# First stage in one written order from the first band means, and a last MLP tile seeded in PSUM: a two-layer diffusion backbone on one core

## Chip, cores and metric

The kernel runs on one core of one Trainium2 chip. The metric is the device time of one execution in microseconds (us); lower is better. Data come in and go out in fp32; products of layers are computed from fp32 values split in a high and a low part of type fp32r (three products each: high by high, high by low, low by high).

## Reference

Two layers over 512 latent tokens (`x`) and 256 context tokens (`ctx`) of width 1024. Layer 0 mixes tokens by pooling, layer 1 by grouped-query attention; each is followed by a squared-ReLU MLP of inner width 4096. Every sub-layer has an RMS norm before and after it, and a shift, scale and gate that a linear map of the conditioning vector gives.

```python
def ada_mods(cond, w, b):
    m = (jax.nn.silu(cond) @ w + b)[..., None, :]
    return jnp.split(m, N_MOD, axis=-1)          # sh1, sc1, gt1, sh2, sc2, gt2

def pool_mixer(h, w_pool, pool_scale):           # windows 2, 4, 8, 16 for four groups of 256 columns
    ...
        mean = (jnp.take(csg, hi, axis=1) - jnp.take(csg, lo, axis=1)) / cnt
        diff = (mean - hf[..., sl]).astype(h.dtype)
        outs.append(diff @ w_pool[g])
    return jnp.concatenate(outs, axis=-1) * pool_scale

for i in range(2):
    h_lat = modulate(rms_norm(x, g_mix_pre[i]), sh1, sc1)          # the same for ctx
    y_lat = pool_mixer(...) if i == 0 else attention_mixer(...)
    x = x + gt1 * rms_norm(y_lat, g_mix_post[i])
    m_lat = sq_relu_mlp(modulate(rms_norm(x, g_mlp_pre[i]), sh2, sc2), w_mlp_in[i], w_mlp_out[i])
    x = x + gt2 * rms_norm(m_lat, g_mlp_post[i])                   # ctx likewise, in layer 0 only
return x
```

## The kernel before

Tokens lie in six tiles of 128 rows (`t` 0 to 3 latent, 4 and 5 context). TensorE (PE) multiplies, VectorE (DVE) and ScalarE (ACT) do the element work, GpSimd (POOL) takes powers for the norms, and SyncE (SP) issues all DMAs in one queue.

**First stage** (all lines of it are recorded as L87, the line of the helper that keeps program order). For each tile: load, `rows_a` (mean square on ACT, then `+ EPS` and the power -0.5 on POOL), `rows_b` (rows scaled, DVE), `band_mm` (products with banded matrices that give "window mean minus identity", PE, tiles `psm` of latent and `psc` of context columns), `band_ev` (out of PSUM, ACT or DVE). Column blocks are numbered `k` 0 to 7; `psm` and `psc` hold two of them. Beside this the conditioning runs: `ada_mm` multiplies a 1 MB load of `w_ada` with the conditioning vectors (tile `psada`), `ada_rows` transposes the result on DVE, `ada_sel` turns it into columns on PE, `ada_mods` adds the bias on DVE. Names such as `SC1_2` mean scale 1, columns from block 2 on; a load of width `w=4` covers four blocks and half of the inner dimension (`a` and `b` halves), one of width 2 covers two blocks and all of it. The products of the means with the pooling weights follow (`pool:t:g`, group `g` needs the blocks 2g and 2g+1, made by `hi:k` on ACT and `lo:k` on DVE), and the chain of each tile: mean square (`ms`), `rs`, copy out (`c`), gate (`b`), residual (`r`), mean square (`s`), `rs2`, scaling (`n`), transposes of tile pairs (`turn:t:q`), modulation (`h:t:q`), split in high and low part (`xhi`, `xlo`), and the first MLP products `in:t:q:f` (six matmuls of 256 columns each, `f` one of two PSUM tiles `psin`). The first unit of the MLP ends with `relu` of both `f`, and PE goes on with the next unit (L608).

Their order is a list by hand: `Steps` sorts the calls by a number `z`. Up to z = 24.5 the calls have their numbers in the code; from there the words of the string `FIRST` give them, one after the other. While `ordered` and `mixed` are on (z 0 to 100), PE, DVE and ACT carry out their instructions in exactly this program order; the SP queue takes its loads in this order as well. Four PSUM buffers `psB` (tag b) and two `psA` (tag a, two banks each) are shared; a tile waits until a buffer is free. Seven buffers take 1 MB loads.

**Middle.** MLP of layer 0, attention, MLP of layer 1 in a loop that is the same before and after; what is not pinned there is ordered by the compiler's own timing.

**Last MLP tile.** `finish` runs `out_mm` (products of the last two units, PE) and `out_ev` (L890: PSUM added to the accumulator `acc`, DVE) for each tile, then `norm_a` (L196: mean square of each column part, ACT; L207, L209, L211: sums and power, POOL), `norm_g` (L361: times gate, DVE) and `fin_b` (L364: residual, DVE; L1495: store). The last tile (`t` = 3) has three column parts, `THIRDS`: 512, 256 and 256 columns; PE does the parts one after the other.

Of the kernel before, what the change touches and what calls it, by code (L numbers as in the profile page):

```python
# [35 lines left out]
CONDITIONING = ((SC1, 0, 4), (SH1, 0, 4), (SC1, 2, 2), (SH1, 2, 2), (SC1, 3, 2), (SH1, 3, 2),  # L36
                (GT1, 0, 4), (GT1, 2, 4), (SC2, 0, 4), (SH2, 0, 4), (SC2, 2, 2), (SH2, 2, 2), (SC2, 3, 2), (SH2, 3, 2))
# [9 lines left out]
rows:GT1_2 ms:4:1 pool:0:2 gate:1:0 c:4:1 rs:4 sel:GT1_2 gate:0:0 pool:0:3 mods:GT1_2 gc:1:1 gc:0:1 whi:0 b:4:0  # L47
psg:1:1 pool:1:0 gate:1:1 wlo:0 psg:0:1 ms:0 b:5 pool:1:1 c:0* mm:SC2_0a rs:0 pool:1:2 r:5 ms:1:0 mm:SC2_0b
gate:0:1 b:4:1 pool:1:3 s:5 r:4 pool:3:0 pool:2:0 ms:1:1 rs2:5 b:0 mm:SH2_0a s:4 pool:3:1 rs:1 r:0 pool:2:1 n:5*
pool:2:2 rs2:4 b:1:0 mm:SH2_0b s:0 b:1:1 pool:3:2 r:1 pool:3:3 n:4* rs2:0 pool:2:3 rows:SC2_0 s:1 turn:4:0  # L50
rows:SH2_0 turn:4:1 sel:SC2_0 n:0* rs2:1 sel:SH2_0 mods:SC2_0 mods:SH2_0 mm:SC2_2 h:4:0 h:4:1* mm:SH2_2 n:1
xhi:4:1 rows:SC2_2 turn:0:0 xhi:4:0 xlo:4:1 turn:0:1 ms:3 xlo:4:0 sel:SC2_2 rows:SH2_2 h:0:0* mods:SC2_2 rs:3
# [38 lines left out]
def backbone(ctx: ExitStack, tc, x, ctx_in, w_ada, w_pool, pool_scale, w_qkv, g_q, g_k, w_o, w_mlp_in,  # L91
# [81 lines left out]
    HALVES, THIRDS = ((0, 512), (512, 512)), ((0, 512), (512, 256), (768, 256))  # L173

# [262 lines left out]
    for v, c in ((0, HALO), (1, P)):  # L437
        ve.tensor_copy(bands[:, v], bands[:, 2])
        ve.tensor_copy(bands[:, v, :, c:c + HALO], edges[:, v])

    means, lat, con = {}, {}, {}

    def band_open(k):
        lat[k] = psA.tile([P, 2, 512], F32, tag="a", name="psm")
        con[k] = psB.tile([P, 2, 256], F32, tag="b", name="psc")
        for u in range(2):
            means[k + u] = lat[k][:, u, :], con[k][:, u, :]
# [18 lines left out]
    def rows_a(t):  # L466
        rs[t] = row_rstd(xr[:, t, :])
# [21 lines left out]
    def pool_weights():  # L489
        for h in range(2):  # L490
            ps = psB.tile([P, 512], F32, tag="b", name="psg")
            te.matmul(ps, one[0:1, 0:1].broadcast_to([1, P]), scale_row[:, 512 * h:512 * h + 512], start=True, stop=True)
            pw.append(ps)
# [308 lines left out]
    def both(ks):  # L802
        for t in range(NL, NT):
            band_mm(t, ks)
# [782 lines left out]
```

## Time and profile before

| what | value |
|---|---|
| median of 3 runs (lowest to highest) | 1163.33 us (1163.19 to 1163.43) |
| time of the profiled execution | 1161.48 us |
| its span (first to last instruction) | 1159.7 us |
| instructions | 15945 |
| busy: PE / DVE / ACT / POOL | 1140.7 / 932.7 / 628.8 / 69.2 us |
| first product of the second MLP unit (L608, end of the first stage on PE) | 96.88 us |
| last residual begins (L364) | 1155.34 us |

A row of the timeline has: start in us, duration in us, engine, line, operation, output<-input, shape, xcount, and in brackets the idle time of the engine before it with what ended it. Rows on one line merge neighbouring instructions of one form. A row of groups has busy time in us and mean ns of one, then idle time before. `PEld` is the weight load of PE, which runs beside its matmuls. Durations of matmuls overlap, since they are pipelined: from start to start is what one costs.

### The profile page before, as it was taken

What the parts mean: (1) busy time and instruction counts of PE and PEld (TensorE: products, weight loads), DVE (VectorE), ACT (ScalarE), POOL (GpSimd) and SP (SyncE); (2) the same over time, 40 slices, a digit from 0 to 9 for tenths busy, and PEclk for the clock granted to TensorE, in tenths of its full rate; (3) what the DMA queues carried; (4) which work ended last, traced back from release to release, by engine and by line L of the source; (5) the groups of instructions that cost most, each with busy time, mean ns of one, the idle gap of its engine ahead of it and who ended that gap; (6) DMA issues with size and microseconds to landing.
All of it is one profiled execution on the core that took longest, in us unless ns stands there. A gap on an engine that the chain in (4) does not pass through costs nothing.

```text
span 1159.7 us, 15945 instructions
## 1 busy us (share of the span) xinstructions
PE 1140.7 (98%) x6172; PEld 990.7 (85%) x6172; DVE 932.7 (80%) x1515; ACT 628.8 (54%) x1068; POOL 69.2 (6%) x120
## 2 busy tenths in 40 slices
PE   7999999999999999999999999999999999999997
PEld 5679889998898988998888889998988888888886
DVE  4688588998988997996777699867687679778876
ACT  5676555554354534555675367753676436534522
POOL 2130000000000000000242200001100000000001
PEclk9999999999999999999999999999999999999999
DMA  9964222443334444343422102125334214313212
GB/s 374 418 270 151 73 99 87 146 145 131 123 145 146 146 146 145 109 146 109 182 73 73 37 1 74 37 74 168 122 146 146 81 64 146 109 44 138 109 41 104
DMA packets 25516, 147.32 MB, mean 127 GB/s; under 512 B 2785, under 2 KB 5217, under 8 KB 9698
## 3 DMA queue, kind: packets, MB, share of 16 engines
q1 hardware_dynamic: 25442, 146.32, 34.4%
q8 instruction: 48, 0.79, 0.3%
q14 instruction: 26, 0.21, 0.1%
HBM read 138.96 MB, written 7.34 MB: 126 GB/s over the span
## 4 chain that ended last, share of the span: by engine, by line
PE 62%; issue 30%; DVE 2%; POOL 2%; ACT 2%; DMA 1%; POOLq 0%; SPq 0%; DVEq 0%; ACTq 0%
PE pso L878 22%; PE psin L732 18%; PE psy L1403 3%; PE po L1378 3%; PE pss L1337 3%; PE psq L1133 2%; PE pspt L1359 2%; PE pspool L87 2%; PE psin L87 1%; PE psin L608 1%; PE psada L87 1%; DMA raw<-in_w_ada 1%; PE psm L87 1%; POOL rs L211 1%; PE psg L87 1%
## 5 line engine op out<-in xcount | busy, mean ns | idle before, releaser
L878 PE MATMUL pso<-units,rb 128*128 128x512 f32 x1152 | 278.8, 392 | 0.0
L878 PEld LDWEIGHTS pso<-units,rb 128*128 128x128 f32 x1152 | 214.7, 188 | 41.1
L301 DVE SCALAR_TENSOR_TENSOR rows<-raw,cond,rows 128x256 f32<-128x256 f32 x280 | 127.2, 478 | 2.0
L890 DVE TENSOR_TENSOR acc<-acc,pso 128x512 f32<-128x512 f32 x129 | 85.4, 676 | 40.5 <-PE pso L878 40.3
L608 PE MATMUL psin<-ra,rb 128*128 128x512 f32 (+1 forms) x310 | 87.8, 360 | 0.0
L987 PE MATMUL pso<-units,pairs 128*128 128x512 f32 x336 | 82.6, 389 | 0.0
L608 PE MATMUL psin<-ra 128*128 128x512 f32 (+1 forms) x256 | 76.5, 376 | 0.0
L987 PEld LDWEIGHTS pso<-units,pairs 128*128 128x128 f32 x336 | 63.1, 188 | 13.1
L991 DVE TENSOR_TENSOR acc<-acc,pso 128x512 f32<-128x512 f32 x72 | 48.7, 682 | 26.2 <-PE pso L987 26.2
L732 PE MATMUL psin<-ra,units 128*128 128x384 f32 x336 | 65.6, 337 | 0.4 <-ACT psin L744 0.4
L209 POOL TENSOR_SCALAR ms<-ss 128x1 f32<-128x1 f32 x16 | 8.7, 541 | 936.6 <-ACT junk L196 922.9
L732 PE MATMUL psin<-sums,units 128*128 128x384 f32 x336 | 64.0, 336 | 0.0
L732 PEld LDWEIGHTS psin<-ra,units 128*128 128x128 f32 x336 | 59.9, 188 | 3.9 <-ACT psin L744 0.5
L608 PEld LDWEIGHTS psin<-ra,rb 128*128 128x128 f32 x310 | 55.6, 189 | 8.7
L169 DVE TENSOR_TENSOR units<-raw,units 128x1024 fp32r<-128x1024 f32 (+2 forms) x49 | 55.1, 1152 | 8.6 <-ACT units L166 8.4
L732 PEld LDWEIGHTS psin<-sums,units 128*128 128x128 f32 x336 | 58.9, 188 | 1.6
L608 PE MATMUL psin<-rb 128*128 128x512 f32 (+1 forms) x155 | 55.8, 361 | 0.6 <-DVE rb L1472 0.6
L166 ACT CAST units<-raw 128x1024 fp32r<-128x1024 f32 (+2 forms) x49 | 46.9, 996 | 17.0 <-PE pso L878 12.9
L608 PEld LDWEIGHTS psin<-ra 128*128 128x128 f32 x256 | 47.1, 188 | 8.8
L888 ACT COPY acc<-pso 128x512 f32<-128x512 f32 x48 | 27.1, 586 | 46.9 <-PE pso L878 46.4
L1133 PE MATMUL psq<-units,ra 128*128 128x512 f32 x216 | 52.2, 393 | 0.0
L608 PE MATMUL psin<-rb,ra 128*128 128x512 f32 (+1 forms) x128 | 48.1, 376 | 0.0
(284 smaller groups left out, 2385.5 us busy)
## 6 DMA issues: line engine op xcount, KB each, us to landing
raw<-in_w_ada SPq DMA_DIRECT2D x48, 1024.0 KB, 5.2
raw<-in_w_mlp_in SPq DMA_DIRECT2D x32, 1024.0 KB, 4.9
raw<-in_w_mlp_out SPq DMA_DIRECT2D x32, 1024.0 KB, 5.8
raw<-in_w_qkv SPq DMA_DIRECT2D x6, 1024.0 KB, 4.9
spill<-xr SPq DMA_DIRECT2D x10, 512.0 KB, 4.3
xr<-spill SPq DMA_DIRECT2D x10, 512.0 KB, 6.7
raw<-in_w_o SPq DMA_DIRECT2D x4, 1024.0 KB, 4.8
xr<-in_x SPq DMA_DIRECT2D x4, 512.0 KB, 5.3
```

Source lines behind the costliest of these rows:

```text
L87: return lambda *args, **kw: self.tc.keep_in_program_order(f(*args, **kw))
L166: a = sc.copy(hi, raw)
L169: b = ve.tensor_tensor(out=lo, in0=raw, in1=hi, op=ALU.subtract)
L301: ve.scalar_tensor_tensor(out=r, in0=raw[:, k, :], scalar=cond[:, k, c:c + 1], in1=r, op0=ALU.mult, op1=ALU.add)
L608: te.matmul(ps[:, bank, o:o + ln], w[:, k, fs], rhs, start=start, stop=(k == KT - 1 and n == 2), skip_group_check=len(ks) < KT or self.paired)
L732: te.matmul(bank, w[k], a[k], start=start and k == 0 and m == 0, stop=stop and k == 3 and m == 2, skip_group_check=True)
L878: te.matmul(pss[h][:, 0:cols[h][1]], a[:, f, ts_], w[:, f, cols[h][0]:sum(cols[h])], start=(n == 0 and not seeded[t]), stop=(n == len(seq) ...
L890: ve.tensor_tensor(out=d, in0=d, in1=ps[:, 0:w], op=ALU.add)
L987: te.matmul(ps, a, w, start=(m == 0), stop=(m == len(seq) - 1))
L991: ve.tensor_tensor(out=M[n][:, t], in0=M[n][:, t], in1=ps, op=ALU.add)
L1133: te.matmul(ps, a[:, k, sl], w[:, k % 4, :], start=(k == 0 and n == 0), stop=(k == KT - 1 and n == 2))
L1337: te.matmul(ps[:, c2, 0:384], a[:, sl], b[:, kv, 384 * c2:384 * c2 + 384], start=(n == 0), stop=(n == 2))
```

## The change

1. *First stage.* `FIRST` now begins at z = 14.5, with the first evacuation of band means (`ev:0`), and has another order. New words: `rb`, `psc0`, `psm`, `psc`, `ev`, `evc` (rows, band products and their evacuations) and `wsc`, `wph`, `wpl` (pool weights scaled and split).
2. `SC1` and `SH1` are loaded for two blocks at a time throughout (`SC1_0`, `SC1_1` in place of `SC1_0` with halves a and b). Bytes and number of loads are the same, the pool weights are now loaded ahead of them.
3. `rows_a` adds `EPS` on DVE in place of POOL, within DVE's program order. Matrices for the last context tile (`band_edge(1)`) are made after two tiles in place of at once; the product that spreads the pool scale (`pool_weights`) is split, half 0 at the start, half 1 between the band products of tiles 1 and 2. `psm` and `psc` are opened apart.
4. *Last tile.* `seeded` is true for it: ACT copies its three parts of `acc` into PSUM ahead of the products, which accumulate on them. `out_ev` does nothing for it. Mean squares and gate products read PSUM; the sum of the three mean squares is one POOL instruction for the first two and one ACT instruction (Identity with a bias) for the third, then the power on POOL.
5. Its residual and store are in parts of 640 and 384 columns (512 and 512 before).

Columns 512, 256 and 256 are the parts that the tile had before as well (`LAST` has the value of `THIRDS`). The diff, with the old list cut:

```diff
-CONDITIONING = ((SC1, 0, 4), (SH1, 0, 4), (SC1, 2, 2), (SH1, 2, 2), (SC1, 3, 2), (SH1, 3, 2),
-                (GT1, 0, 4), (GT1, 2, 4), (SC2, 0, 4), (SH2, 0, 4), (SC2, 2, 2), (SH2, 2, 2), (SC2, 3, 2), (SH2, 3, 2))
+CONDITIONING = ((GT1, 0, 4), (GT1, 2, 4), (SC2, 0, 4), (SH2, 0, 4),
+                (SC2, 2, 2), (SH2, 2, 2), (SC2, 3, 2), (SH2, 3, 2))
 FIRST = """
-psc45 ev6 mm:SH1_0a ev4c psc67 mm:SH1_0b ev6c rows:SH1_0 mm:SC1_2 sel:SH1_0 rows:SC1_2 mods:SH1_0 sel:SC1_2 hi:0
-mods:SC1_2 mm:SH1_2 hi:1 lo:0 hi:2 rows:SH1_2 lo:1 mm:SC1_3 hi:3 sel:SH1_2 lo:2 pool:5:0 pool:4:0 rows:SC1_3
-mods:SH1_2 sel:SC1_3 lo:3 hi:5 mm:SH1_3 mods:SC1_3 hi:4 pool:5:1 rows:SH1_3 lo:5 sel:SH1_3 mm:GT1_0a pool:4:1
-mods:SH1_3 lo:4 hi:6 pool:0:0 pool:0:1 hi:7 lo:6 mm:GT1_0b pool:5:2 ms:4:0 lo:7 pool:4:2 c:4:0* rows:GT1_0
-mm:GT1_2a pool:5:3 sel:GT1_0 ms:5 pool:4:3 mods:GT1_0 gc:1:0 gc:0:0 psg:1:0 c:5* rs:5 mm:GT1_2b w_in psg:0:0
...
-rs2:2 sel:SH2_3 mods:SC2_3 in:0:2:0 mods:SH2_3 h:4:3 in:0:2:1 n:2* h:0:3 in:4:2:1 xhi:4:3 turn:2:0 turn:2:1
-xhi:0:3 xlo:4:3 turn:2:2 h:2:1* h:2:0 turn:2:3 in:4:3:0 xhi:2:1 xlo:0:3 in:4:3:1 xhi:2:0 xlo:2:1 in:0:3:0 h:2:2*
-xlo:2:0 in:2:1:0 h:2:3 xhi:2:2 in:2:0:0 in:2:0:1 xlo:2:2 xhi:2:3 in:2:1:1 xlo:2:3 in:2:2:1 in:0:3:1 in:2:2:0
-in:2:3:0 in:2:3:1
+ev:0* ev:2 psc0:4 psm:4 rb:5 wsc:0 psm:6 wsc:1 ev:4* wph:0 mm:SC1_0 wph:1 wpl:0 mm:SH1_0 ev:6* rows:SC1_0 wpl:1
+psc0:5 sel:SC1_0 rows:SH1_0 evc:2* mods:SC1_0 evc:0* sel:SH1_0 mm:SC1_1 mods:SH1_0 hi:0 psc:4 rows:SC1_1 hi:1
+psc:6 lo:0 mm:SH1_1 evc:4* lo:1 evc:6* sel:SC1_1 rows:SH1_1 pool:4:0 mods:SC1_1 sel:SH1_1 mm:SC1_2 mods:SH1_1
+hi:2 pool:0:0 rows:SC1_2 pool:5:0 hi:3 lo:2 mm:SH1_2 lo:3 sel:SC1_2 rows:SH1_2 pool:4:1 mods:SC1_2 sel:SH1_2
+ms:4:0 mm:SC1_3 mods:SH1_2 hi:4 c:4:0 pool:5:1 rows:SC1_3 mm:SH1_3 hi:5 lo:4 sel:SC1_3 pool:0:1 rows:SH1_3
+mods:SC1_3 sel:SH1_3 lo:5 pool:1:0 pool:1:1 mods:SH1_3 pool:5:2 hi:6 mm:GT1_0a ms:1:0 lo:6 pool:4:2 hi:7
+mm:GT1_0b c:1:0 lo:7 pool:0:2 mm:GT1_2a rows:GT1_0 pool:4:3 sel:GT1_0 ms:4:1 mm:GT1_2b w_in mods:GT1_0 gc:0:0
+gc:1:0 c:4:1* rs:4 pool:0:3 rows:GT1_2 psg:0:0 ms:0 sel:GT1_2 psg:1:0 c:0* mods:GT1_2 rs:0 gc:0:1 gc:1:1 psg:1:1
+gate:1:0 gate:0:0 pool:5:3 b:4:0 gate:1:1 b:1:0 mm:SC2_0a ms:5 b:4:1 psg:0:1 r:4 c:5* rs:5 pool:1:2 gate:0:1 b:5
+mm:SC2_0b s:4 pool:1:3 r:5 whi:0 rs2:4 pool:3:0 ms:1:1 rows:SC2_0 pool:3:1 c:1:1* b:0 mm:SH2_0a rs:1 n:4*
+sel:SC2_0 b:1:1 mm:SH2_0b s:5 r:0 pool:2:0 whi:1 rs2:5 pool:2:1 rows:SH2_0 pool:2:2 s:0 mods:SC2_0 r:1 sel:SH2_0
+mm:SC2_2 n:5* rs2:0 mods:SH2_0 wlo:0 pool:2:3 s:1 turn:4:0 n:0 turn:4:1 ms:2 rs2:1 mm:SH2_2 h:4:1 h:4:0* rs:2
+pool:3:2 n:1 xhi:4:0 mm:SC2_3 rows:SH2_2 xhi:4:1 rows:SC2_2 xlo:4:0 sel:SH2_2 turn:0:1 xlo:4:1 sel:SC2_2 h:0:1*
+pool:3:3 mods:SH2_2 mods:SC2_2 turn:0:0 b:2 xhi:0:1 mm:SH2_3 ms:3 xlo:0:1 in:4:0:1 h:0:0* rows:SH2_3 rs:3
+in:4:1:1 b:3 xhi:0:0 in:0:1:1 r:3 turn:0:2 in:4:0:0 h:0:2* xlo:0:0 in:4:1:0 s:3 r:2 in:0:1:0 in:0:0:1 xhi:0:2
+rs2:3 wlo:1 s:2 in:0:0:0 turn:0:3 xlo:0:2 n:3* sel:SH2_3 rs2:2 turn:4:2 rows:SC2_3 in:0:2:0 mods:SH2_3 h:4:2*
+n:2 sel:SC2_3 in:0:2:1 xhi:4:2 mods:SC2_3 turn:2:2 h:0:3 turn:4:3 h:2:2* turn:2:3 xlo:4:2 turn:2:1 xhi:2:2 h:4:3
+in:4:2:1 h:2:1* in:4:2:0 xlo:2:2 xhi:4:3 h:2:3 turn:2:0 in:2:2:1 xhi:2:1 xlo:4:3 xhi:0:3 in:2:2:0 xlo:2:1 h:2:0*
+in:4:3:1 xlo:0:3 in:2:1:0 xhi:2:0 xhi:2:3 in:0:3:1 xlo:2:0 xlo:2:3 in:0:3:0 in:4:3:0 in:2:0:0 in:2:3:0 in:2:0:1
+in:2:3:1 in:2:1:1
 """
+    LAST = ((0, 512), (512, 256), (768, 256))
 ...
     def rows_a(t):
-        rs[t] = row_rstd(xr[:, t, :])
+        ss, ms, rs[t] = sm_tile("ss"), sm_tile("ms"), sm_tile("rs")
+        mean_square(xr[:, t, :], ss[:, 0:1])
+        ve.tensor_scalar(out=ms[:, 0:1], in0=ss[:, 0:1], scalar1=EPS, scalar2=None, op0=ALU.add)
+        gp.tensor_tensor(out=rs[t][:, 0:1], in0=ms[:, 0:1], in1=nhalf[:, 0:1], op=ALU.pow)
 ...
+    st.at(0.1, pool_weights, 0)
+    for k in (0, 2):
+        st.at(1, band_open, k)
+        st.at(1, band_open_c, k)
     for t in range(NT):
         st.at(4.6 + 1.3 * t, rows_a, t)
-    for t, z in enumerate((7.8, 9.7, 11.2, 12.7, 14.2, 16)):
-        st.at(z, rows_b, t)
 ...
+    for t in range(NL + 1):
+        st.at(5.5 + 1.3 * t, rows_b, t)
     for t in range(NL):
+        st.at(5.6 + 1.3 * t, band_mm, t, range(4))
+    st.at(7.9, pool_weights, 1)
+    st.at(6.85, band_edge, 1)
+    st.at(14, pool_load)
 ...
-        st.at(24.5 + n / 1000, step, what)
+        st.at(14.5 + n / 1000, step, what)
 ...
-        seeded[t] = i == 0 and parts[0][0] > 0 and len(parts) == 1 and t in (1, 4) and stale[0] <= 0
+        seeded[t] = cols == LAST or i == 0 and parts[0][0] > 0 and len(parts) == 1 and t in (1, 4) and stale[0] <= 0
 ...
-                sc.copy(ps, accv[:, t, c0:c0 + w])
+                sc.copy(ps[:, 0:w], accv[:, t, c0:c0 + w])
 ...
     def out_ev(i, parts, t, cols=HALVES):
+        if cols == LAST:
+            return
 ...
+    def last_rstd(t, ss):
+        ms, rs[t] = sm_tile("ms"), sm_tile("rs")
+        for n, (c0, w) in enumerate(LAST):
+            mean_square(pso[t][n][:, 0:w], ss[:, n:n + 1])
+        gp.tensor_scalar(out=ms[:, 0:1], in0=ss[:, 0:1], scalar1=ss[:, 1:2], scalar2=EPS, op0=ALU.add, op1=ALU.add)
+        sc.activation(ms[:, 1:2], ss[:, 2:3], AF.Identity, scale=1.0, bias=ms[:, 0:1])
+        gp.tensor_tensor(out=rs[t][:, 0:1], in0=ms[:, 1:2], in1=nhalf[:, 0:1], op=ALU.pow)
 ...
     def norm_g(t, pool=False, cols=HALVES):
         yg[t] = work_tile()
-        for c0, w in cols:
-            z = gated(t, yg[t], accv[:, t, c0:c0 + w], c0, c0 + w, pool)
-            if cols == THIRDS:
+        for n, (c0, w) in enumerate(cols):
+            z = gated(t, yg[t], pso[t][n][:, 0:w] if cols == LAST else accv[:, t, c0:c0 + w], c0, c0 + w, pool)
+            if cols == LAST:
                 tc.keep_in_program_order(z)
 ...
-        for n0, n1 in ((0, 512), (512, D)):
+        c = 640 if t == NL - 1 else 512
+        for n0, n1 in ((0, c), (c, D)):
```

More of the change, by code (lines that the diff above doesn't have):

```diff
@@ L48 @@
[L48 to L52, printed above, removed]
@@ L436, in backbone, with band_edge @@
     edges = gflat[:, 12 * BW:12 * BW + 64].rearrange("p (v g n) -> p v g n", v=2, g=4)
-    for v, c in ((0, HALO), (1, P)):
+    def band_edge(v):
+        c = (HALO, P)[v]
         ve.tensor_copy(bands[:, v], bands[:, 2])
         ve.tensor_copy(bands[:, v, :, c:c + HALO], edges[:, v])
+    band_edge(0)
     means, lat, con = {}, {}, {}
@@ L444, in band_open, with band_open_c @@
         lat[k] = psA.tile([P, 2, 512], F32, tag="a", name="psm")
+        for u in range(2):
+            means[k + u] = lat[k][:, u, :], None
+    def band_open_c(k):
         con[k] = psB.tile([P, 2, 256], F32, tag="b", name="psc")
         for u in range(2):
-            means[k + u] = lat[k][:, u, :], con[k][:, u, :]
+            means[k + u] = means[k + u][0], con[k][:, u, :]
     def band_mm(t, ks):
@@ L487, in backbone, with pool_weights @@
     pw = []
[L489 to L493, printed above, removed]
+    def pool_weights(h):
+        ps = psB.tile([P, 512], F32, tag="b", name="psg")
+        te.matmul(ps, one[0:1, 0:1].broadcast_to([1, P]), scale_row[:, 512 * h:512 * h + 512], start=True, stop=True)
+        pw.append(ps)
     def pool_load():
@@ L797, in conditioning, with band_rows, band_context @@
         m, j = dict(SH1=SH1, SC1=SC1, GT1=GT1, SH2=SH2, SC2=SC2)[m], int(j[0])
-        w = 4 if j == 0 or m == GT1 else 2
+        w = 4 if m == GT1 or j == 0 and m in (SC2, SH2) else 2
         zs = (("ab".index(what[-1]),),) if w == 4 and fn == ada_mm else ()
         fn(0, m, j, *((w, *zs) if fn == ada_mm else ()))
-    def both(ks):
+    def band_rows(k):
+        band_open(k)
+        for t in range(NL):
+            band_mm(t, (k, k + 1))
+    def band_context(k):
+        band_open_c(k)
         for t in range(NL, NT):
-            band_mm(t, ks)
+            band_mm(t, (k, k + 1))
     def split_w(h, part):
@@ L823, in backbone @@
     kinds = dict(
-        psc45=lambda: both((4, 5)), psc67=lambda: both((6, 7)), ev6=lambda: band_ev(6, 0, True),
-        ev4c=lambda: band_ev(4, 1, True), ev6c=lambda: band_ev(6, 1, True),
+        rb=rows_b, psc0=lambda t: band_mm(t, range(4)), psm=band_rows, psc=band_context,
+        ev=lambda k, act: band_ev(k, 0, act), evc=lambda k, act: band_ev(k, 1, act),
+        wsc=pool_scaled, wph=lambda h: pool_split(h, True), wpl=lambda h: pool_split(h, False),
         mm=lambda x: conditioning(ada_mm, x), rows=lambda x: conditioning(ada_rows, x),
@@ L1174, in norm_a @@
         ss = sm_tile("ss")
+        if cols == LAST:
+            return last_rstd(t, ss)
         for n, (c0, w) in enumerate(cols):
@@ L1497, in last1 @@
     def last1(st, n, t):
-        cols = THIRDS if t == NL - 1 else HALVES
+        cols = LAST if t == NL - 1 else HALVES
         st.at(5.2 * n + 5.3, norm_a, t, cols)
```

25 lines of the change are left out of this document (3 added, 22 removed).

## Prediction

> **What bounds the kernel now.** I read the page first, then PE's waits, then the windows of ten us, then the rows at both ends of the run.
>
> ```profile
> span 1159.7 us, 15945 instructions
> ...
> PE 1140.7 (98%) x6172; PEld 990.7 (85%) x6172; DVE 932.7 (80%) x1515; ACT 628.8 (54%) x1068; POOL 69.2 (6%) x120
> ```
>
> PE is busy all but 19 us. In the profiled execution (1161.48 us, 1.8 beyond its span; the median of the runs is 1.85 above it) only two places can give time back without taking work from PE: the first stage and the tail. PE's waits from 8.6 to 97 us (total, times, longest):
>
> ```profile
> PE psada L87 <- DMA raw<-in_w_ada: 2.5, 3, 1.4
> PE psada L87 <- DVE mods L87: 1.5, 3, 0.7
> PE psada L87 <- ACT acc L87: 0.7, 1, 0.7
> PE psin L608 <- ACT work L615: 0.2, 1, 0.2
> ```
>
> That is 4.9 us, the ceiling for a mere change of order. The same view from 97 to 1150 us has five rows that sum to 2.2 us, the first and last of them:
>
> ```profile
> PE pss L1337 <- ACT gate L1342: 0.6, 2, 0.4
> ...
> PE psin L608 <- ACT work L615: 0.2, 1, 0.2
> ```
>
> So PE goes on without a break once the stage is over, and what it gains at the start should arrive at the end. The stage's other limit is DMA (columns: PE, PEld, DVE, ACT, POOL busy, clock, DMA share, GB/s):
>
> ```profile
> 60.00:70.00 10.00, 9.78 (x107) 7.14 (x109) 6.11 (x11) 7.36 (x13) 3.91 (x9) 1.00 1.01 417
> 70.00:80.00 10.00, 9.27 (x120) 6.98 (x113) 9.96 (x19) 9.45 (x18) 2.28 (x4) 1.00 0.21 83
> ```
>
> Loads run at full rate until about 70 us: 1.05 MB each, so 2.5 us apart at 417 GB/s. Neither their number nor the rate changes, so their landing times are given.
>
> **First stage: the waits taken out.** PE's rows in order of time:
>
> ```profile
> 31.07 1.07 PE L87 MATMUL psada<-raw,cond 128*32 128x256 f32 x16 [0.62 <-DMA raw<-in_w_ada]
> 33.55 1.07 PE L87 MATMUL psada<-raw,cond 128*32 128x256 f32 x16 [1.41 <-DMA raw<-in_w_ada]
> 34.41 0.25 PE L87 MATMUL psada<-rows,sel 128*32 128x4 f32 x8
> ```
>
> ```profile
> 42.86 1.69 PE L87 MATMUL pspool<-rb,ra 128*128 128x256 f32 x12
> 44.49 1.06 PE L87 MATMUL psada<-raw,cond 128*32 128x512 f32 x8
> ```
>
> A load's product costs 1.0 us, a pooling group (6 of the 12 matmuls that fill 42.86 to 44.49) 0.8, a turn into columns (`sel`) 0.25. PE waits for loads here because it has nothing else to do: the old `SC1_0` and `SH1_0` need two loads each before any block has its scale and shift. In the new list blocks 0 and 1 have both after the second conditioning load, so pooling groups stand between the later loads.
>
> A load that PE waited for landed when its row starts: `SH1_2` at 31.07, `SC1_3` at 33.55, and 2.5 later, at 36.05, `SH1_3`. That holds in the new order too, as the same nine loads (pool weights and eight of `SC1` and `SH1`) come first in both. After `SH1_3` the new list has its product 1.0, two turns 0.5, groups 0:1, 1:0, 1:1 and 5:2 3.2 (at 40.75), then `GT1_0a`, 4:2, `GT1_0b`, 0:2, `GT1_2a`, 4.6 more: done at 45.35, with eleven groups behind it. Before, `GT1_2a` is done at 45.5 (44.49 and 1.0) with eight. The lead is three groups and 0.15 us, 2.5 us, provided PE is ready for `SH1_3` when it lands. Two turns more than before (`SC1_1`, `SH1_1`, 0.5 us) are in this.
>
> **First stage: what is added at its start.** PE's rows:
>
> ```profile
> 4.98 3.75 PE L87 MATMUL psg<-work,sm 1*128 1x512 f32 x4 [4.98 <-DMA work<-in_pool_scale]
> 8.66 6.60 PE L87 MATMUL psm<-gate,acc 128*128 128x136 f32 x32
> 15.10 1.09 PE L87 MATMUL psc<-gate,acc 128*128 128x136 f32 x8
> ```
>
> The weight loads of one tile's eight band products, from the row of PEld:
>
> ```profile
> 10.19 1.99 PEld L87 LDWEIGHTS psm<-gate,acc 128*128 128x128 f32 x8
> ```
>
> And the rows of x on DVE, the power on POOL, the first copy of means on ACT, and, for want of a one-column add on DVE, its nearest row, the reciprocal of one column:
>
> ```profile
> 12.52 0.75 DVE L87 TENSOR_SCALAR acc<-xr,rs 128x1024 f32<-128x1024 f32 x1 [0.76 <-POOL rs L211]
> 14.04 0.75 DVE L87 TENSOR_SCALAR acc<-xr,rs 128x1024 f32<-128x1024 f32 x1 [0.77 <-POOL rs L211]
> ```
>
> ```profile
> 13.44 0.57 POOL L211 TENSOR_TENSOR rs<-ms,nhalf 128x1 f32<-128x1 f32 x1
> ```
>
> ```profile
> 14.83 1.01 ACT L87 COPY acc<-psm 128x1024 f32<-128x1024 f32 x1 [1.11 <-PE psm L87]
> ```
>
> ```profile
> L1348 DVE RECIPROCAL sm<-sm 128x1 f32<-128x1 f32 x32 | 5.1, 158 | 1.3 <-ACT gate L1342 0.3 <-ACT acc L1342 0.3 <-ACT p L1342 0.3
> ```
>
> Rows of x come 1.52 us apart now. With the add of `EPS` on DVE in program order, tile t+1's add stands behind tile t's scaling and ahead of its own: a chain of add 0.16, power 0.57, scaling 0.75 and hand-overs, 1.55 to 1.65 us a tile. What waits behind the add on DVE is the scaling, and for that PE waits. Tile 3 comes 0.1 to 0.4 us later by this, and by up to 0.75 (bounded by a scaling) for `band_edge(1)`, which now lies between tiles 1 and 2; in return tile 0 no longer has it ahead.
>
> PE is slower yet. Eight weight loads took 1.99 us at 10.19, while the eight `psc` products of 15.10 have full pace, 0.12 each (1.09 with the last one's run-out): PE is at half pace until about 13 us, though the clock column of the windows shows 1.00 from the start. The spreading product costs 0.94 a matmul cold (3.75 for four). New order: tile 0 from 8.4, tile 1 until 12.4 cold, `pool_weights(1)` until 13.4 if warm or 14.3 if cold, tiles 2 and 3 about 1.0 each until 15.3 to 16.2, against the copy's start at 14.83. I take 1.0 us late, from the middle of the two. About half of it comes through, since the landings at 31 to 36 us stay: the lead is 2.0 us. Bounds: 0.2 lost, or a PE that stays cold through tile 3, which is the first rival.
>
> [...]
>
> **First stage: its end.** From 45 us on both lists hold the same products, and PE is full but for 1.2 us (two of the waits for `mods`, 1.0, and L615's 0.2).
>
> ```profile
> 86.10 1.91 PE L87 MATMUL psx<-ident,acc 128*128 128x128 f32 x16
> 87.76 8.87 PE L87 MATMUL psin<-ra,rb 128*128 128x256 f32 x72
> 96.88 16.91 PE L608 MATMUL psin<-ra,units 128*128 128x384 f32 x96 [0.25 <-ACT work L615]
> ```
>
> Twelve `in` products take 8.7 us, 0.72 each; a transpose pair of `turn` 0.42 (1.66 for four). The wait ahead of L608 goes: `f` 0 now ends with three products of `f` 1 behind it, 2.2 us in which ACT can empty it, where one product, 0.72, left 0.25 open. The waits for `mods` may go or come back elsewhere; I count nothing. Stage: 2.0 and 0.25, say 2.3 us, L608 at 94.6. Bounds: 0 and 4.4 (every wait less the two turns).
>
> **The tail.** What stands around the last tile on DVE and ACT, then its own chain:
>
> ```profile
> 1146.62 1.37 DVE L890 TENSOR_TENSOR acc<-acc,pso 128x512 f32<-128x512 f32 x2 [0.76 <-PE pso L878]
> ```
>
> ```profile
> 1147.40 0.63 ACT L196 ACTIVATE junk<-acc 128x512 bf16<-128x512 f32 x1 [4.04 <-DVE acc L890]
> ```
>
> ```profile
> 1152.88 0.42 DVE L890 TENSOR_TENSOR acc<-acc,pso 128x256 f32<-128x256 f32 x1 [0.51 <-PE pso L878]
> ```
>
> ```profile
> 1153.44 0.42 ACT L196 ACTIVATE junk<-acc 128x256 bf16<-128x256 f32 x1
> ```
>
> ```profile
> 1154.11 0.55 POOL L209 TENSOR_SCALAR ms<-ss 128x1 f32<-128x1 f32 x1 [0.15 <-POOL ss L207]
> 1154.75 0.56 POOL L211 TENSOR_TENSOR rs<-ms,nhalf 128x1 f32<-128x1 f32 x1
> 1155.34 1.42 DVE L364 SCALAR_TENSOR_TENSOR xr<-work,rs,xr 128x512 f32<-128x512 f32 x2 [0.76 <-POOL rs L211]
> ```
>
> From PE's last product (1152.88) to the residual (1155.34) lie 2.46 us: add, square, sum, power. New: the square reads PSUM at once, from 1152.93; its sum is there 0.62 later (0.67 from 1153.44 to POOL's start, less a hand-over). Then the one-column Identity on ACT in place of POOL's 0.55: no row shows it just so; it lies between the reciprocal's 0.16 and the square's 0.42, and I take 0.2, near the former for its one column. 1152.93 + 0.62 + 0.2, a hand-over of 0.05, power 0.56 and 0.03 put the residual at 1154.4: 0.9 us gained. Residual and store are as long in sum; the last store is a quarter smaller, counted at nothing. Bounds 0.3 to 1.2.
>
> The seeds are three ACT copies, 0.63, 0.42 and 0.42 by ACT's rows of these widths. ACT's idle 4.04 us before 1147.40 covers the first two; the third needs a buffer that DVE frees from 1146.62 on, and has two parts' products ahead of it. Without that cover, the first seed queued behind tile 2's square, PE would stand still for 1.8 us at about 1147.
>
> Square and gate product of a part now read one PSUM tile. In the view of the tile `psy`, whose parts are read by both as well, ACT's squares waited for DVE's gate products (us, times):
>
> ```profile
>   ACT junk L196: 11.7, 6
> ```
>
> [...] Here the square is written first, and the gate product has until 1154.4: I count none of it.
>
> Sum: 2.3 + 0.9 = 3.2 us. The profiled 1161.48 becomes 1158.3, the median 1163.33 becomes 1160.1. A measurement of this kernel can tell about 0.2% (2.3 us) from no change, so faster is below 1161.0.
>
> **Rivals.**
>
> *Cold clock* (0.17). PE stands idle for 1.5 us after the first spreading product, the second one (one row of PE wide) falls into the middle, and PE isn't released before tile 3 is done. Tiles 2 and 3 cost 2.0 each: first means at 18.3, 2.1 us later than I take, of which 1.6 comes through. Stage 0.7, with the tail 1.6: 1161.7. For it: the spreading products ahead of 8.66 didn't warm PE. Against it: dense work from 8.4 to 12.4.
>
> *Only the tail gains* (0.12). PE comes to each load late and the lead is lost: 1162.4; the seeds' stall would do as much in another place. Against it: the eleven groups' operands need no load after `SH1_3`.
>
> *Slower* (0.13), by the row chain of tile 3, whose last pooling group now stands behind `SC2_3`.
>
> ```profile
> 65.03 2.42 PE L87 MATMUL pspool<-rb,ra 128*128 128x256 f32 x18
> ```
>
> ```profile
> 47.39 1.05 PE L87 MATMUL psg<-ident,gc 128*128 128x128 f32 x8
> ```
>
> Before, this group ends at 67.4 and the pair's transposes begin at 86.10, 18.7 us later. New: from 45.35 and 0.5 for the start, thirteen groups, eight loads, six turns, four gate spreads (1.0 each) and four transposes put it at 71.5. Fourteen `in` products and five transposes, 12.2 us, stand from `turn:2:2` on, so that decides from 84.7. With the old 18.7 us it begins at 90.2, L608 at 102.4: 5.5 later, less the tail's 0.9: 1167.9. For it: DVE and ACT are 99% and 94% busy from 70 to 80. Against it: much of the 18.7 was queueing behind other tiles, and `ms:3`, `b:3` and `r:3` now follow the product closely; I expect 81 to 82.
>
> That the change of order does nothing is no rival: the order is binding on PE, DVE and ACT.
>
> **Numbers.** Forecast 0.58, cold clock 0.17, tail alone 0.12, slower 0.13. Some nine in ten of the forecast's cases (stage 1.5 to 4) and a few of the cold ones lie below 1161.0: faster 0.57, same 0.30, slower 0.13. The range leaves out the slower rival and the last of the ceiling: 1158.0 to 1163.4.
>
> **What would show it.** Right: the first copy of `psm` near 16 us; no wait of PE for `in_w_ada` above 0.5 us; L608 near 94.6; the residual 1.5 us behind PE's last product; no L890 in tile 3. Wrong: weight loads at half pace beyond 14.5 us; PE waiting for `acc` ahead of tile 2's transposes; L878 waiting for ACT in the last tile; new waits of PE between 97 and 1150 us.

## The result and the profile after

The changed kernel takes 1159.99 us in the median of 12 runs (1157.69 to 1161.33), the kernel before 1163.01 us beside it (12 runs, 1161.78 to 1164.28). The ratio is 0.9971, 95% interval 0.9963 to 0.998: 3.0 us less. The profiled execution of the changed kernel took 1160.61 us, with a span of 1158.8. From the page:

```profile
span 1158.8 us, 16048 instructions
...
PE 1142.9 (99%) x6220; PEld 992.7 (86%) x6220; DVE 932.9 (81%) x1522; ACT 632.8 (55%) x1076; POOL 69.7 (6%) x113
```

PE has 2.2 us more busy time than before and the span is 0.9 us shorter. PE's waits from 4 to 97 us show what has gone:

```profile
PE psg L89 <- DMA work<-in_pool_scale: 5.1, 1, 5.1
PE psm L89 <- DVE acc L89: 2.0, 2, 1.1
PE psg L89 <- DVE gc L89: 0.3, 1, 0.3
```

The 5.1 us is the wait for the first load, as before. The waits for `in_w_ada` (2.5 us), for `mods` (1.5) and for `acc` of ACT (0.7) are gone, and so is the 0.25 ahead of the MLP unit. In their place stand 2.0 us ahead of the band products of tiles 0 and 1, and something that no view of waits shows. PE's rows at the start:

```profile
8.06 2.18 PE L89 MATMUL psm<-gate,acc 128*128 128x136 f32 x8 [0.90 <-DVE acc L89]
11.36 2.29 PE L89 MATMUL psm<-gate,acc 128*128 128x144 f32 x8 [1.12 <-DVE acc L89]
13.58 2.07 PE L89 MATMUL psg<-work,sm 1*128 1x512 f32 x2
15.58 3.87 PE L89 MATMUL psm<-gate,acc 128*128 128x144 f32 x16
19.29 1.09 PE L89 MATMUL psc<-gate,acc 128*128 128x136 f32 x8
20.22 3.98 PE L89 MATMUL psm<-gate,acc 128*128 128x136 f32 x32
```

Eight products take 1.9 to 2.3 us until 19 us and 1.09 after it: TensorE is at half pace for all four latent tiles, and the spreading product between tiles 1 and 2 takes 2.07 us. So the first means are copied 4.0 us later than before, and the second MLP unit, L608 before and L621 now, begins only 0.3 us earlier than in the profile of before:

```profile
18.81 1.01 ACT L89 COPY acc<-psm 128x1024 f32<-128x1024 f32 x1 [3.96 <-PE psm L89]
```

```profile
96.58 16.81 PE L621 MATMUL psin<-ra,units 128*128 128x384 f32 x96
```

At the other end of the run the chain of the last tile is short, and no DVE addition (L904 now) stands in it:

```profile
1151.73 0.88 PE L890 MATMUL pso<-units 128*128 128x256 f32 x6
1152.70 0.38 ACT L199 ACTIVATE junk<-pso 128x256 bf16<-128x256 f32 x1 [0.96 <-PE pso L890]
1153.01 0.20 ACT L199 ACTIVATION_READ_ACCUMULATOR junk<-pso 128x1 f32 x1
1153.25 0.42 DVE L364 TENSOR_TENSOR work<-pso,gate 128x256 f32<-128x256 f32 x1 [0.93 <-ACT junk L199]
1153.31 0.29 ACT L1200 ACTIVATE ms<-ss,ms 128x1 f32<-128x1 f32 x1
1153.68 0.56 POOL L1201 TENSOR_TENSOR rs<-ms,nhalf 128x1 f32<-128x1 f32 x1 [1.54 <-ACT ms L1200]
1154.28 1.42 DVE L367 SCALAR_TENSOR_TENSOR xr<-work,rs,xr 128x640 f32<-128x640 f32 x2 [0.61 <-POOL rs L1201]
```

PE's last product ends at 1152.61 and the residual begins 1.67 us later, where it was 2.46. From 97 to 1150 us PE's waits are the old ones (1.9 us in sum, 2.2 before).

The two profiles differ by 0.9 us and the medians by 3.0. Where the other 2 us are had to come from experiments.

### The profile page after: what moved, and what is told of

Read it like the earlier page. It is cut to its first block, busy times and chain, and to the rows that moved or that the text cites. A ratio compares the mean times of both kernels' runs of the same rounds, so it can differ in the third digit from the quotient of the medians.

```text
span 1158.8 us, 16048 instructions
## 1 busy us (share of the span) xinstructions
PE 1142.9 (99%) x6220; PEld 992.7 (86%) x6220; DVE 932.9 (81%) x1522; ACT 632.8 (55%) x1076; POOL 69.7 (6%) x113
## 3 DMA queue, kind: packets, MB, share of 16 engines
q1 hardware_dynamic: 25442, 146.32, 34.8%
## 4 chain that ended last, share of the span: by engine, by line
PE 91%; issue 2%; DVE 2%; ACT 2%; POOL 2%; DMA 1%; SPq 0%; POOLq 0%; DVEq 0%; ACTq 0%
PE pso L890 24%; PE psin L745 18%; PE psin L621 16%; PE pso L1001 12%; PE psy L1427 3%; PE po L1402 3%; PE pss L1361 3%; PE psq L1147 2%; PE pspt L1383 2%; PE pspool L89 2%; PE psada L89 2%; PE psin L89 2%; PE psm L89 1%; PE psx L89 1%; PE psg L89 1%
## 5 line engine op out<-in xcount | busy, mean ns | idle before, releaser
L904 DVE TENSOR_TENSOR acc<-acc,pso 128x512 f32<-128x512 f32 x126 | 84.0, 682 | 40.8 <-PE pso L890 40.7
L621 PE MATMUL psin<-ra,rb 128*128 128x512 f32 (+1 forms) x310 | 87.8, 360 | 0.0
L621 PE MATMUL psin<-ra 128*128 128x512 f32 (+1 forms) x256 | 76.5, 376 | 0.0
L621 PEld LDWEIGHTS psin<-ra,rb 128*128 128x128 f32 x310 | 55.6, 189 | 8.7
L621 PE MATMUL psin<-rb 128*128 128x512 f32 (+1 forms) x155 | 55.8, 361 | 0.6 <-DVE rb L1496 0.6
L621 PEld LDWEIGHTS psin<-ra 128*128 128x128 f32 x256 | 47.1, 188 | 8.8
L621 PE MATMUL psin<-rb,ra 128*128 128x512 f32 (+1 forms) x128 | 48.1, 376 | 0.0
```

Of the source, the lines that this page charges most:

```text
L621: te.matmul(ps[:, bank, o:o + ln], w[:, k, fs], rhs, start=start, stop=(k == KT - 1 and n == 2), skip_group_check=len(ks) < KT or self.paired)
L904: ve.tensor_tensor(out=d, in0=d, in1=ps[:, 0:w], op=ALU.add)
```

## The experiments

Three theories of what sets the gain of the first stage. **Clock**: PE goes through from 20 us on without waiting, so its time up to there is handed through, and that time depends on how long TensorE stays at half pace. **Rows**: the scaled rows of x (squares on ACT, `EPS` on DVE, power on POOL) set the start. **Loads**: the landings of the weights set the stage, and what PE loses at the start is mostly absorbed. Medians of before beside these runs were 1162.9 (the four kernels e1, e2, e4, e5), 1162.71 (e0, e3, e6, e7) and 1163.09 (e8 to e11).

**The parts apart.** e1 is the kernel before with the tail of the change alone (`LAST`, the seeds, `last_rstd`, the residual cut at 640); e2 is the changed kernel without it:

```diff
-            cols = LAST if (i, t) == (1, NL - 1) else HALVES
+            cols = THIRDS_ if (i, t) == (1, NL - 1) else HALVES
```

(in both places that choose the columns, and with the residual cut at 512; `THIRDS_` holds the three parts, and `LAST` is `None` there).

> The kernel before with the last tile's change alone (seeds, mean squares and gate products from PSUM, Identity, residual in 640 and 384 columns). By the prediction's sum 0.9 us less. By the trace of the changed kernel the residual begins 1.67 us behind PE's last product in place of 2.46 (0.8 us), of which the end of the span shows 0.65: 0.65 to 0.8 us less. If the tail's gain needs the new order: no change. First stage as before: first copy of band means near 14.8 us, next unit's first product near 96.9.

> The changed kernel with the old last tile: the first stage's new order alone. Theory clock: the gain depends on when TensorE is released from half pace, in some runs near 13 us (4 us gained), in others at 19 us (0.3 us gained); median 2.0 to 2.5 us less than before, single runs spread over 3 us or more. Theory loads (the landings alone set the stage's end): 2.5 us in every run, spread under 1 us. Theory tail alone: under 0.5 us.

e1 took 1161.57 us (11 runs, 1161.09 to 1163.82), ratio 0.9991 [0.9982, 0.9999]; e2 1160.92 us (11 runs, 1158.84 to 1161.79), ratio 0.9981 [0.9972, 0.9989]. By the ratios that is 1.0 us (interval 0.1 to 2.1) and 2.2 us (1.3 to 3.3), by the medians 1.3 and 2.0: the two parts add up, and neither needs the other. e2's runs spread over 3.0 us, as clock expected, and not under 1, as loads did. e1's stage did not repeat the profile of before, as it was expected to: its first means are copied at 15.21, not near 14.8, and its next unit starts 2.3 us late, for a reason shown below. From the start of the second MLP unit to the end of the span it is 1062.2 us in `after` (1158.8 - 96.58) and 1062.1 in e1 (1161.3 - 99.18), 1062.8 in `before` and 1063.0 in e2: the tail's gain is 0.6 to 0.9 us between any two of these traces, and all else is decided by when that unit starts. In e2 PE's rows are those of the same first stage, in another run:

```profile
7.85 4.60 PE L89 MATMUL psm<-gate,acc 128*128 128x136 f32 x16 [1.08 <-DVE acc L89]
12.38 2.07 PE L89 MATMUL psg<-work,sm 1*128 1x512 f32 x2
14.38 3.56 PE L89 MATMUL psm<-gate,acc 128*128 128x144 f32 x16
17.78 1.09 PE L89 MATMUL psc<-gate,acc 128*128 128x136 f32 x8
18.70 3.98 PE L89 MATMUL psm<-gate,acc 128*128 128x136 f32 x32
```

The means of groups 4 to 7 start at 18.70 instead of 20.22, and L621 at 95.03 instead of 96.58: 1.52 and 1.55 us, one for one.

e1 shows something of the kernel *before* that its own profile didn't. Its windows (PE, PEld, DVE, ACT, POOL busy, clock, DMA share, GB/s):

```profile
30.00:32.00 2.00, 0.95 (x30) 0.63 (x20) 0.99 (x5) 0.48 (x1) 0.00 (x0) 1.00 1.01 422
32.00:34.00 2.00, 1.07 (x16) 0.50 (x16) 1.64 (x4) 2.00 (x5) 0.00 (x0) 1.00 0.99 414
34.00:36.00 2.00, 1.43 (x16) 0.96 (x20) 1.97 (x4) 2.00 (x5) 0.00 (x0) 0.70 1.03 426
36.00:38.00 2.00, 2.00 (x20) 1.95 (x13) 1.59 (x5) 1.31 (x3) 0.00 (x0) 0.50 1.01 422
38.00:40.00 2.00, 2.00 (x31) 1.27 (x31) 0.47 (x4) 1.61 (x3) 0.00 (x0) 0.94 1.03 410
```

While PE waits for loads it is half busy from 30 to 34 us, and the clock falls to 0.50 from about 35 to 38. Its row there, against the same row of before at 34.59 with 1.69 us:

```profile
36.33 2.53 PE L87 MATMUL pspool<-rb,ra 128*128 128x256 f32 x12
```

Its second MLP unit starts at 99.18, where the profile of before has 96.88. e5, which has the order of before too, shows the same fall for longer, from 33.8 to 40.7 us.

How often this happens can be read from the mean granted clock, which is on record for each of 65 runs of the kernel before (those beside e0 to e11). e1's traced run has 0.997. 27 of the 65 have 0.997 or less, and their median is 1163.55 us; the other 38 have 1162.30. All 23 runs of the changed kernel (the result and e0), and all 11 of e2, have 0.998 or more. The mean of the 65 is 1162.99, that of the 38 is 1162.38, so some 0.6 us of the 3.0 would be falls of the clock that the new order doesn't have. A mean doesn't tell where in a run the clock fell: that it is this place in each of the 27 is not shown.

**The changed kernel again, and the spreading product moved.** e0 is the changed kernel. e3 writes both one-row spreading products ahead of tile 0, e8 the second one behind tile 3:

```diff
-    st.at(7.9, pool_weights, 1)
+    st.at(0.2, pool_weights, 1)      # e3
+    st.at(9.6, pool_weights, 1)      # e8
```

> The changed kernel once more, for a second trace and to stand beside the next three on the same chip. 2.5 to 3.5 us less than before, single runs 1157.5 to 1161.5. Theory clock: its first copy of means comes the later the longer TensorE's weight loads stay at half pace (0.33 us), between 15.5 and 19 us, and each us there costs 0.7 us or more at the next unit's first product.

> The changed kernel with the second spreading product right behind the first one instead of between the band products of tiles 1 and 2. Theory clock: at half pace that product took 2.0 us in the middle; ahead of tile 0 it lies in idle time, so the first copy comes 1 to 2 us earlier (near 17 where the clock stays low) and the time is 0.7 to 1.5 us below the changed kernel's. Theory rows: no difference, as TensorE waits for the rows anyway.

> The changed kernel with the second spreading product behind the band products of the fourth latent tile, instead of between the second and the third. Clock theory (PE waits for nothing from 20 us on, so its time up to there is handed through to the end, and a spreading product costs 2.07 us at half pace and 1.1 at full pace): the band products are no longer parted by the one-row product, PE is released before the fourth tile ends, the product costs 1.1 us; L621 begins near 95, median 1158.0 to 1159.0, beside 1158.0 with both spreading products ahead. If the product only costs 2.07 us in another place: 1160.4, as the changed kernel. Rows theory (the scaled rows of x set the start): 1160.4 as well, and the first means a little earlier.

e0: 1160.4 us (11 runs, 1157.88 to 1161.65), ratio 0.9978 [0.9969, 0.9987]; its means of groups 4 to 7 start at 20.30 and L621 at 96.65, 76.35 us apart, as in `after` (76.36) and e2 (76.33). e3: 1158.02 us (5 runs, 1157.56 to 1158.97), ratio 0.9962 [0.9948, 0.9975], 2.4 below e0 where clock expected 0.7 to 1.5. Its rows:

```profile
4.96 3.75 PE L89 MATMUL psg<-work,sm 1*128 1x512 f32 x4 [4.96 <-DMA work<-in_pool_scale]
8.63 2.18 PE L89 MATMUL psm<-gate,acc 128*128 128x136 f32 x8
11.57 5.58 PE L89 MATMUL psm<-gate,acc 128*128 128x144 f32 x24 [0.76 <-DVE acc L89]
16.99 1.09 PE L89 MATMUL psc<-gate,acc 128*128 128x136 f32 x8
17.92 3.98 PE L89 MATMUL psm<-gate,acc 128*128 128x136 f32 x32
```

The second product holds tile 0 back by 0.7 us (8.63, 7.92 in e0), but that is taken out of PE's wait for the rows of tile 1, and tiles 1 to 3 run through without a one-row product among them. The means of groups 4 to 7 start 2.4 us earlier than in e0, though x's second tile landed a microsecond later in this run; L621 begins at 94.96, 1.7 us earlier (0.5 is lost in a wait for `ra` of DVE at 37.45). That speaks against rows: tile 3's rows are scaled at 14.31, 13.28 in e0, and yet the means come earlier. Of the 23 runs of the changed kernel 18 took longer than the longest of e3.

e8: 1159.25 us (5 runs, 1157.8 to 1159.57), ratio 0.9963 [0.995, 0.9976]. In its profiled run, the longest of the five:

```profile
10.93 6.16 PE L89 MATMUL psm<-gate,acc 128*128 128x144 f32 x24 [0.60 <-DVE acc L89]
17.02 1.18 PE L89 MATMUL psg<-work,sm 1*128 1x512 f32 x2
18.13 1.19 PE L89 MATMUL psc<-gate,acc 128*128 128x136 f32 x8
19.16 3.98 PE L89 MATMUL psm<-gate,acc 128*128 128x136 f32 x32
```

The product costs 1.18 us at full pace, as clock expected, the median lies 0.25 above what it expected, and 19.16 to L621 at 95.52 is 76.36 us again. So the place between tiles 1 and 2 is the dear one: there the product took 2.07 us (`after`, e0, e2), and it parts the band products.

**TensorE warmed.** e4 is the changed kernel, e5 the kernel before, each with ten products of the identity by itself ahead of the first spreading product. e6 (changed kernel, both spreading products first) and e7 (before) have such products between the tiles too, 9, 4, 5, 3 and 2 at the five places:

```diff
+    def warm_up(n):
+        for z in range(n):
+            te.matmul(con[0][:, 0, 0:P], ident, ident, start=True, stop=True)
...
+    for z, n in ((0.05, 9), (0.3, 4), (5.65, 5), (6.95, 3), (8.25, 2)):
+        st.at(z, warm_up, n)
```

> The changed kernel with ten products of the identity with itself (128 columns, result unused) ahead of the first spreading product, at a time when TensorE has nothing else to do. Theory clock: weight loads at full pace (0.19 us) from the first or second band product on, first copy of means near 15.8 us in place of 18.8 (bound by the rows of x), next unit's first product near 94 in place of 96.6, every run within 1 us of the others and near the fastest of the changed kernel, 1157.5. Theory rows (the rows of x, late by the add on VectorE, set the start): first copy not before 18, time near 1160. Theory loads: first copy early, but next unit still near 96.5.

> The kernel before with the same ten products ahead of its spreading products. Theory clock: its first copy of means can come at most 0.4 us earlier (rows of x are done at 13.3 us), and its next 20 us wait for loads whatever the start, so 0 to 0.7 us less in the median and runs closer together. If warmth alone were worth the gain of the changed kernel: 2 us less or more.

> The changed kernel with products of the identity (128 columns, into a PSUM tile that is overwritten later) not only ahead of the first spreading product (9) but behind it (4) and behind the band products of tiles 0, 1 and 2 (5, 3, 2), and the second spreading product right behind the first. Theory clock: TensorE stays at full pace from about 6 us on, all band products have weight loads of 0.19 us, first copy near 15.8 (bound by tile 3's rows at 14.8), next unit's first product near 94, 1157.0 to 1157.8 in most runs. Theory rows or loads: full pace, but next unit at 95.5 or later, 1159.5 or more.

> The kernel before with the same products of the identity ahead of, behind and between. Theory clock: full pace too, first copy near 14.5 to 15.5 in every run, but its first 20 us run into the landings of the loads, so 0 to 1 us less than before. If full pace at the start were what the new order lives on, 2 us less or more.

e4: 1160.3 us (11 runs), ratio 0.9979 [0.997, 0.9988], as the changed kernel. Warmth ahead doesn't last:

```profile
5.76 1.12 PE L89 MATMUL psg<-work,sm 1*128 1x512 f32 x2
8.12 1.41 PE L89 MATMUL psm<-gate,acc 128*128 128x136 f32 x8 [1.24 <-DVE acc L89]
10.04 2.29 PE L89 MATMUL psm<-gate,acc 128*128 128x144 f32 x8 [0.51 <-DVE acc L89]
12.26 2.07 PE L89 MATMUL psg<-work,sm 1*128 1x512 f32 x2
```

The spreading product and most of tile 0 are at full pace, and at 10 us TensorE is at half pace again; the expected gain was missed. e5: 1162.11 us (11 runs, 1161.39 to 1165.06), ratio 0.9998 [0.9989, 1.0007], nothing, and its runs are not closer together, as clock expected. Its profiled run is the longest; there the clock fell again at 9.9 us, in a wait of 1.80 ahead of tile 1, and the first means are copied at 16.25.

e6: 1158.51 us (5 runs, 1157.83 to 1159.69), ratio 0.9967 [0.9955, 0.998]. Its tiles are at full pace throughout, 1.09 to 1.25 us each; the first means are copied at 15.02 and groups 4 to 7 start at 16.76, 1.2 us ahead of e3. L625, its second MLP unit, begins at 94.49, between what clock expected (94) and what the others did (95.5), and the median is 0.7 above what clock expected. In its trace the loads bind now. PE's waits after 20 us:

```profile
PE psada L89 <- DMA raw<-in_w_ada: 0.9, 2, 0.5
PE psg L89 <- DVE gc L89: 0.3, 1, 0.3
PE psada L89 <- DVE mods L89: 0.2, 1, 0.2
```

e7: 1163.11 us (11 runs), ratio 1.0002 [0.9993, 1.0011]. It doesn't test what it was for: in its profiled run the four one-row products took 3.78 us and TensorE was cold until some 13.7 us (tile 0's eight products 2.02 us, tile 1's 1.15). But it shows the other half: its first means are copied at 18.16, 3.3 us later than in the profile of before, and its second MLP unit starts 1.6 us later, with 0.3 us of waits for loads left of 2.5. In this pair of traces the loads of the kernel before do absorb half of a late start.

**The row chain and the loads.** e9 is e3 with the addition of `EPS` back on POOL. e10 (changed kernel) and e11 (e6) load half of the pooling weights and set the other half to zero, so they leave out a part of the result:

```diff
-        ss, ms, rs[t] = sm_tile("ss"), sm_tile("ms"), sm_tile("rs")
-        mean_square(xr[:, t, :], ss[:, 0:1])
-        ve.tensor_scalar(out=ms[:, 0:1], in0=ss[:, 0:1], scalar1=EPS, scalar2=None, op0=ALU.add)
-        gp.tensor_tensor(out=rs[t][:, 0:1], in0=ms[:, 0:1], in1=nhalf[:, 0:1], op=ALU.pow)
+        rs[t] = row_rstd(xr[:, t, :])                                    # e9
...
-        pw[0:0] = raw_load(w_pool, rawp), wpH, wpL
+        t = rawp.tile([P, 2048], F32, tag="raw", name="raw")             # e10, e11
+        tc.keep_in_program_order(sy.dma_start(t[:, 0:1024], w_pool[:, 0:1024]))
+        gp.memset(t[:, 1024:2048], 0.0)
+        pw[0:0] = t, wpH, wpL
```

> Both spreading products ahead (1158.02 us), and the addition of EPS for the rows of x back on POOL, 0.55 us in place of 0.15 us on DVE and a hand-over. Clock theory: the rows of x come 0.3 to 0.5 us later each, PE is behind them for part of the tiles only; 1158.0 to 1158.5. Rows theory: the full step in each of the six rows, 1.5 us or more by the third tile: 1159.5 or above.

> The changed kernel with only half of the pooling weights loaded (the other half is set to zero on POOL), so that every later load lands 1.25 us earlier. Clock theory: PE waits for no load in the changed kernel, so nothing: 1160.0 to 1160.6, L621 near 96.5 in a run with the first means at 18 to 19. Loads theory (landings set the stage): 1159.1, a full 1.25 us less.

> The version whose TensorE is kept at full pace from 1.3 us on (1158.51 us; PE waits 0.9 us for two loads at 34 to 37 us), with half of the pooling weights loaded. If its limit has become the landing of loads: the two waits go and L625 begins at 93.6 instead of 94.49; median 1157.4 to 1157.8. If something else limits it: 1158.5, as without the edit.

e9: 1157.91 us (5 runs, 1157.56 to 1158.67), ratio 0.9959 [0.9947, 0.9971], no different from e3. Its rows of x come 1.51 us apart (12.37, 13.88, 15.40), those of `after` 1.48 (14.09, 15.57), not the 1.5 us that rows expected by the third tile. Where `EPS` is added doesn't matter here. As the edit hardly moves the rows, it doesn't show what later rows would cost; against rows as what sets the time speaks e3.

e11: 1158.04 us (5 runs, 1157.56 to 1160.99), ratio 0.9963 [0.9951, 0.9975]. In its profiled run, the shortest, both waits for loads are gone and the second MLP unit starts at 93.34 (expected 93.6), 1.15 us ahead of e6. That answers to loads binding in e6; the median moved by only 0.5 (1157.4 to 1157.8 was expected) and is no better than e3's, and why is not shown.

e10: 1157.9 us (7 runs, 1156.75 to 1162.05), ratio 0.9962 [0.9949, 0.9975]. Both expectations missed: nothing was due by clock, 1.25 us by loads, and it is 2.1 to 2.5 us below the changed kernel's two medians. The runs lie in two groups, four from 1156.75 to 1157.9 and three from 1160.61 to 1162.05. The profiled one is the longest, and it is cold for long, with no wait for a load:

```profile
15.95 4.10 PE L89 MATMUL psm<-gate,acc 128*128 128x144 f32 x16
19.84 1.80 PE L89 MATMUL psc<-gate,acc 128*128 128x136 f32 x8
21.48 2.78 PE L89 MATMUL psm<-gate,acc 128*128 128x136 f32 x22
```

From 21.48 to its L624 at 97.84 it is 76.36 us. Of the short runs there is no trace, so why this edit gives more of them stays open.

## Why the prediction was right, and where not

The time (1160.1 forecast, 1159.99 measured) and the split into 2.3 us for the stage and 0.9 for the tail (e2 2.2, e1 1.0 by their ratios) came out. The steps did so less well, the stage's above all: that its 2.3 us fits is luck, as two errors of like size cancel in it.

*The lead.* Right in what it removes: no wait for `in_w_ada` or `mods` is left, L621 waits for nothing, and no new one came between 97 and 1150 us. But its proviso failed, that PE is ready for `SH1_3` when it lands. In `after` PE comes to that product at 39.25 us; I reckoned with a landing at 36.05, and e6, which waits for it, has it at 37.16. So `GT1_2a` is done at 48.5, where I had 45.35.

*The start.* The step that failed. I put the first copy of means at 16 us with a PE that is released during tile 1 or soon after, an estimate from the one trace I had. Already the release in the profile of before I read too early: its weight loads take 0.34 us until 13.8, not 13, which is 5.1 us after the first band product. The traces of this stage have 18.81 (`after`), 18.00 (e0) and 17.51 (e2), with the second spreading product at the cold price, 2.07, in all three. That is the *cold clock* rival, whose 18.3 lies amid them and to which I gave 0.17; its time, 1161.7, is 1.7 us too long all the same, since it has the same fault at the other end (below, under L608).

*"About half of it comes through, since the landings stay."* Wrong for this kernel. In six traces of the changed order the means of groups 4 to 7 start between 18.70 and 21.48 us (`after`, e0, e2, e4, e8, e10), and the second MLP unit follows 76.33 to 76.38 us later in each: all of a late start comes through, as PE has work from 20 us on and waits for no load. In e9 (17.35) and e3 (17.92) the unit follows 76.56 and 77.04 us later. Landings bind where these means start at 16.76, in e6 (0.9 us of waits for two loads). The half fits e7, the one late start of the kernel before that was traced without a fall of the clock.

*L608 at 94.6.* The two profiled runs have 96.58 and 96.65. With 1062.2 us from there to the end of the span and 1.8 beyond it, the median of 1159.99 puts it at 96.0; with 1062.8, the median of before, 1163.01, puts its L608 at 98.4, not at the 96.88 of its profile. So both ends of my subtraction lie 1.4 to 1.5 us too early, and the difference of 2.3 us is right by that alone. On the one side that is the cold start. On the other side the profile of before was a short run: 1161.48 is 1.5 below its median. I saw that offset and carried it over as a constant; e1 shows one thing behind it, a clock that falls to 0.50 at 35 us after the waits for loads, which the profile of before doesn't have. `after`, e0 and e2 have neither these waits nor the fall after 20 us, so a gain lies here that no row of my profile showed, some 0.6 us if the low clocks on record are such falls. The rest of the offset, from 1161.48 to the 1162.30 of the runs whose clock is 0.998 or more, stays open.

*`EPS` on DVE.* 0.15 us a tile against my 0.16; but the chain is 1.48 us a tile and not 1.55 to 1.65, shorter than before, not longer.

*The tail.* From PE's end to the residual 2.46 became 1.67, 0.8 gained for a forecast of 0.9: the Identity took 0.29 where I took 0.2. A further 0.1 went after the residual, where the last store was counted at nothing: span less L621 shows 0.6 to 0.7. The gate product did wait for the square (0.93 us) and was in time. The seeds were hidden, and PE waited for none.

*The slower rival.* The last pooling group of tile 3 ends at 73.5 in `after` (forecast 71.5), sixteen transposes stand at 84.33, 11 us behind and not 18.7, and PE waits for none of them. Refuted, and not narrowly: in e11 PE comes to these transposes at 81.10 and waits for none of them either. *Only the tail gains* is refuted by e2.

A version better than both kernels came out: e3, or e9, 1158.02 and 1157.91 us (5 runs each), by one step's place.

## What to carry to other kernels

Work that was moved to the head of this stage met a TensorE at half pace (tile 0's eight products 2.18 us in `after`, the same number 1.09 from 19.29 us on): price the first 15 to 20 us by the cold rows, keep the dense products together, and put one-row products where PE stands still anyway (e3, 1158.02 us, beside e0's 1160.4). A profile of before is one draw; look where its time stands among the runs before subtracting from its rows, and ask which irregular losses the change also removes. Whether a late start is absorbed depended here on whether loads or PE bind behind it: of e7's 3.3 us half came through, with load waits down from 2.5 us to 0.3, and in the six traces of the changed order without load waits all of it did. The new order removed the load waits, and the absorber with them.

## What the runs showed of the hardware

*One-row products did not bring TensorE to full pace* in these traces. 3.75 us of them lie ahead of tile 0 in e3, and tile 0's eight products still took 2.18 us. In e4, after 4.5 us of dense identity products, 1.12 us of one-row products and a pause of 1.24, the clock column falls to 0.50 at 9.0 us, and tile 1's eight products take 2.29 us. e6 and e7 begin with the same 4.2 us of identity products. In e6 the four one-row products behind them take 2.20 us, and tile 0's eight 1.09. In e7 the four take 3.78, and though PE works on without a pause, it is cold until some 13.7 us, 4.5 us after dense products begin again. Why the two differ is not shown.

*When full pace comes differs from run to run.* In twelve traces (all but e6 and e11) the weight loads fall from 0.33 to 0.19 us between 2.9 us (e2: from 14.38) and some 6 us (e8: from 10.93) after the last pause or one-row product; `after` 3.4, e0 and e10 5.3. The moments at which the clock changes can be worked out from the clock column, by the mean of the 2 us in which it changes (0.74 from 8 to 10 us of e4, between 1.00 and 0.50: it falls at 9.0). They lie at 9.0 and 19.2 in e4, at 9.9, 16.8, 33.8 and 40.7 in e5, at 34.8 and 38.2 in e1: 10.2, 6.8, 17.1, 6.8 and 3.4 us apart, each a whole multiple of some 3.4. Where these moments lie against the last break is not the same in each run, and what sets them is not shown. A stage that goes through without waiting hands this on: 76.33 to 76.38 us from the means of groups 4 to 7 to the second MLP unit in six traces. That fits the spread of the changed kernel's runs, 3.6 us, and the 1.4 of e3 (5 runs), whose tiles no one-row product parts; no short run of the changed kernel was traced. In e1 the fall at 34.8 us came after 4 us (30 to 34) in which PE was busy 2.0 us, and the longest pause, up to 34.58, was 1.41.

*The clock column shows 1.00 through the half pace at the start.* From 5 to 20 us it does so in `after` and e0, while eight products take 2.18 to 2.29 us; there the durations of like products tell. A fall from full pace it does show: 0.66 in the same window of e4, and 0.50 in e1 from 36 to 38 us.
